# The first 512 rows of x turned by the host, their norm applied at the products' exit; u in four tensors; small tables in one input

## The chip, the cores and the metric

The kernel runs on one core of one Trainium2 chip. A core has a matrix engine (PE, with its weight loads shown apart as PEld), a vector engine (DVE), an activation engine (ACT), a general engine (POOL) and a synchronising engine (SP), which here only issues DMAs. Operands lie in an on-chip memory of 128 partitions; products are summed in eight banks that PE writes and DVE and ACT read. Inputs, the output and scratch tensors lie in the chip's main memory, and DMAs move them.

The metric is the device time of one execution in microseconds (us). The time before is 1565.41 us, the median of three runs (1563.84 to 1569.05).

## The reference

One layer on x (2048 rows of 1024, f32). It is cut here to what the change touches.

```
hn = rmsnorm(x, mix_norm_g)                  # x * rsqrt(mean(x*x) + eps) * g, by row
u, g_ssm, q, k, v, g_attn = split(hn @ w_in) # six times 512 columns
y_ssm = s5(u, a, b, c, d, log_dt) ...        # 32 groups of 16 channels, scanned over the rows
y_ssm = y_ssm * silu(g_ssm)
y_att = stick_breaking(q, k, v) * silu(g_attn)
h = x + concat(y_ssm, y_att) @ w_out
out = h + sigmoid(rmsnorm(h, ple_norm_g) @ w_ple_gate) * (p @ w_ple_proj)
```

The norm of a row is a factor by row, and g is a factor by column of x, that is by row of w_in. So `hn @ w_in` is `rs * (x @ (g * w_in))` with rs the reciprocal root of one row.

## The kernel before, in words

**Split numbers.** A product of f32 accuracy is made of three products in a faster format: each operand is split into a high part (a rounded copy, written by ACT) and a low part (the rest, by DVE), and `mm3` adds high x high, high x low and low x high. `split` does this for activations. `load_w` does it for weights: it loads 128 rows of 512 columns into a staging tile `wst`, multiplies by the column of g (`gmix`) and writes both parts. With `act=True` ACT writes the high part, else DVE.

**First stage, `phase_u`.** The rows are taken in eight units T of 256 rows, each of two tiles of 128. `load_x` brings a tile in by rows (512 KB), ACT squares it and sums by row, DVE and POOL make the reciprocal root (`rms_rstd`; the power is POOL's), ACT scales the tile, PE turns it by 16 transposes of 64 x 64 blocks into two banks, and ACT and DVE split the turned tile into `xt`, which SP also writes out as `hn` (1 MB a tile) for the later stages. `u` of a unit is four column tiles ct of eight row blocks c: 96 products, 24 for each ct. In T = 0 the loop over c is outside, so that products can start with the first weights; in the others ct is outside. ACT copies each finished ct to a tile `uq`, and after each odd T POOL issues one DMA of `uq` (1 MB) to the scratch tensor `u`, laid out as 16 steps x 512 channels x 128 chunks. Two `uq` tiles take turns.

**Tables, `ssm_chain`.** The decay, rotation and power tables of the scan are made from small inputs by some hundreds of short DVE instructions, in the time of the first stage. The inputs come in ten small DMAs on POOL's queue; a and c are turned by PE, halves of b and c are exchanged by ACT.

**Second stage.** Eight batches of the scan (`ssm_pack`, `ssm_batch`; four groups each) run against the gates of the eight units (`gate_unit`, 96 products a unit, units 6 and 7 first since their `xt` are still there) and the first projections of attention (`attn_proj`). A batch reads its channels of `u` by one view, `by_channel`, in the DMA to `us`. As there is one tensor `u`, the first batch's read waits for the last write. From 333 us on come attention and the output, which make up the rest.

**The order of the work** isn't the order of the text. `arrange` takes the whole program, estimates each instruction (`duration`), plans each engine's order by a list schedule with ranks from a backward pass, tries six times, and ties each engine to the best order found. Hints: instructions inside `e.first()` are ranked ahead of all others in the order of the text; DMAs inside `e.later()` don't start before the instruction at `e.mark()` has started, which is the first product of T = 2. Each engine then works strictly in its order: an instruction that waits holds up all behind it on the same engine or queue.

Of the kernel before, what the change touches and what calls it, by code (L numbers as in the profile page):

```python
# [18 lines left out]
P = 128  # L19
# [21 lines left out]
XB, XTB, GTB, QSB, BEB, PXB, WSB, SWB, ROTB, STA, STB, STC, ALT, ALT0, ALT1, SSM_STEPS, SSM_DEPTH, PREP0, BEX, PXX, WSX, XTX, XT0 = 3, 2, 5, 5, 6, 4, 5, 2, 2, 3, 2, 3, "o", 0, 30, 10, 2, 0, 0, 0, 0, 0, 13  # L41
# [8 lines left out]
HOLD = 2  # L50
MATB = 1
GSB = 2
NTAB = 3 * KIN + 3 * MOUT + 1

# [117 lines left out]
def ssm_chain(e, keep, sm):  # L172
# [16 lines left out]
    nre = sm.tile([G, P], F32, tag="nre", name="nre")  # L189
    nim = sm.tile([G, P], F32, tag="nim", name="nim")  # L190
    dma = e.cdma
    ldt = t("ldt")
# [3 lines left out]
    dma(ldt, e.log_dt[0].partition_broadcast(P))  # L196
    dsk = R.dsk = kt("dsk", [G])
    nc.gpsimd.memset(dsk[96:], 0.0)
    lr, li = t("lr"), t("li")
    for src, dst in ((nre, lr), (nim, li)):  # L200
        ps = e.bank("ps_prep", "ssm", "tr")
        nc.tensor.transpose(ps[:, :G], src, e.ident[:G, :G])
        nc.vector.tensor_copy(dst, ps[:, :G])
# [3 lines left out]
    br, bi = (b[0].rearrange("g p h -> p g h") for b in (e.b_re, e.b_im))  # L207
    dma(bst[:ST], br)
    dma(bst[ST:], bi)
    nc.scalar.activation(bsw[:ST], bst[ST:], AF.Copy)  # L210
    nc.scalar.activation(bsw[ST:], bst[:ST], AF.Copy)
    cn1 = sm.tile([P, 4, P], F32, tag="cn", name="cn1")
    cr, ci = (c[0].rearrange("g h p -> (g h) p").rearrange("(k r) p -> r k p", r=P) for c in (e.c_re, e.c_im))
    dma(cn1[:, :, :ST], cr)
    dma(cn1[:, :, ST:], ci)
    dma(dsk[P - GH:], e.d_skip[0].rearrange("g h -> h g"))
    R.cts = kt("cts", [G, GH])
    R.ct2 = kt("ct2", [G, GH])
    ps = e.bank("ps_prep", "ssm", "tr")
    for k in range(4):  # L220
        nc.tensor.transpose(ps[:, k * P:(k + 1) * P], cn1[:, k, :], e.ident)
    c2 = R.ct2.rearrange("p g h -> p (g h)")
    nc.scalar.activation(c2[:ST], ps[ST:], AF.Copy)
    nc.scalar.activation(c2[ST:], ps[:ST], AF.Copy)
    vs(nc, R.cts.rearrange("p g h -> p (g h)"), ps, sgn, ALU.mult)
# [39 lines left out]
    tb = sm.tile([P, G, GH], F32, tag="cn", name="tb")  # L265
# [116 lines left out]

def ssm_batch(e, pool, mb, mc, b):
# [4 lines left out]
    nc.sync.dma_start(us.rearrange("p s k c -> p s (k c)"), by_channel(e.u_d, b))  # L388
# [91 lines left out]
def load_w(e, blocks, width, scale, tag="w", pool=None, bufs=None, at=0, act=True):  # L480
# [67 lines left out]
def phase_u(e, pool, xp, chain):  # L548

    nc = e.nc  # L550

    def load_x(T):
# [17 lines left out]
    with e.first():  # L570
        xts[0] = load_x(0)
        w = load_w(e, row_blocks(e.w_in[0], NC8, 0), 512, e.gmix, act=False)
        xts[1] = load_x(1)
    prep = chain()
    for T in range(NT // 2):
        if 2 <= T + 1 < NT // 2:
            xts[T + 1] = load_x(T + 1)
        xt = xts.pop(T - 2, None)
        xt = xts[T]
        if T % 2 == 0:  # L580
            uq = pool.tile([P, L, 4, NCH // 4], F32, tag="uq", name="uq", bufs=2)
        ps = [e.bank("ps_u", "w0", "w1", "o", "acc")[:, :256] for _ in range(4)]
        if T == 2:
            e.mark()
        for ct, c in [(ct, c) for c in range(NC8) for ct in range(4)] if T == 0 else [(ct, c) for ct in range(4) for c in range(NC8)]:
            cs = slice(ct * P, (ct + 1) * P)
            mm3(e, ps[ct], (w[c][:, 0, cs], w[c][:, 1, cs]), (xt[:, :, 0, c], xt[:, :, 1, c]), c == 0, c == NC8 - 1)
        for ct in range(4):
            k0 = (T % 2) * (NCH // 8)
            nc.scalar.activation(uq[:, :, ct, k0:k0 + NCH // 8], ps[ct].rearrange("p (c j) -> p j c", j=L), AF.Copy)  # L590
        if T % 2 == 1:
            c0 = (T // 2) * (NCH // 4)
            nc.gpsimd.dma_start(e.u_d[:, :, c0:c0 + NCH // 4].rearrange("j (k p) c -> p (j k) c", p=P), uq.rearrange("p j k c -> p (j k) c"))
# [3 lines left out]
def gate_unit(e, pool, w, T, xt):  # L597
# [6 lines left out]
    for ct in range(4):  # L604
        o = e.bank("ps_sg", "o", "z0", "z1")[:, :256]
        for c in range(NC8):
            cs = slice(ct * P, (ct + 1) * P)
            mm3(e, o, (w[c][:, 0, cs], w[c][:, 1, cs]), (xt[:, :, 0, c], xt[:, :, 1, c]), c == 0, c == NC8 - 1)
        sg = pool.tile([P, 256], F32, tag="sg", name="sg", bufs=2)
        nc.scalar.activation(sg, o, AF.Sigmoid)  # L610
# [52 lines left out]
def attn_proj(e, pool, A, i, xt=None):  # L663
# [8 lines left out]
    if len(e.q_banks) == 1:  # L672
# [3 lines left out]
        nc.scalar.activation(flat, pq[:, :384], AF.Copy)  # L676
        nc.vector.tensor_copy(vf, pq[:, 384:])
    else:
# [8 lines left out]
        nc.scalar.activation(part, pq[0], AF.Copy)  # L687
        vt(nc, flat, pq[1][:, :384], part[:, :384], ALU.add)
        vt(nc, vf, pq[1][:, 384:], part[:, 384:], ALU.add)
# [285 lines left out]
def hybrid_block_kernel(ctx: ExitStack, tc: tile.TileContext, x, p, mix_norm_g, w_in, ssm_a_re, ssm_a_im, ssm_log_dt,  # L975
                        ssm_b_re, ssm_b_im, ssm_c_re, ssm_c_im, ssm_d, ssm_w_glu, ssm_b_glu, q_norm_g, k_norm_g,
                        w_out, ple_norm_g, w_ple_gate, w_ple_proj, out, rows, pools, dbg=None):
# [3 lines left out]
    e.x, e.p, e.w_in, e.w_glu, e.w_out, e.w_pg, e.w_pp, e.out = x, p, w_in, ssm_w_glu, w_out, w_ple_gate, w_ple_proj, out  # L981
    e.a_re, e.a_im, e.log_dt, e.d_skip = ssm_a_re, ssm_a_im, ssm_log_dt, ssm_d
    e.b_re, e.b_im, e.c_re, e.c_im = ssm_b_re, ssm_b_im, ssm_c_re, ssm_c_im
# [11 lines left out]
    e.u_d = scratch("u", [L, 512, NCH])  # L995
# [19 lines left out]
    nc.vector.memset(e.mhalf, -0.5)  # L1015

    def column(name, src, n=NC8):
        t = const(name, [P, n])
        nc.sync.dma_start(t, src.rearrange("(c p) -> p c", p=P))
        return t  # L1020

    e.gmix = column("gmix", mix_norm_g[0])

    def late_consts():
        e.gple = column("gple", ple_norm_g[0])
        e.bglu = column("bglu", ssm_b_glu[0])
        e.gqk = const("gqk", [P, 1])
        gk = const("gk", [P, 1])
        for half in range(2):
            d = slice(64 * half, 64 * half + 64)  # L1030
            nc.sync.dma_start(e.gqk[d], q_norm_g[0].unsqueeze(1))
            nc.sync.dma_start(gk[d], k_norm_g[0].unsqueeze(1))
# [40 lines left out]
    e.first, e.later, e.mark = (lambda: hint("first")), (lambda: hint("later")), (lambda: rows.append((len(nc.cur_bb.bb.instructions), 0, "mark")))  # L1073
# [10 lines left out]
    gx = pool(left, "gx")  # L1084
    early = ExitStack()
# [14 lines left out]
    attn_w(e, A[0], 0, NC8)  # L1100
# [405 lines left out]
```

## Time and profile before

| what | us |
|---|---|
| median of three runs | 1565.41 |
| lowest, highest | 1563.84, 1569.05 |
| the profiled execution's own time | 1566.84 |
| its span, first to last instruction | 1565.1 |
| first stage, to the last product of u | 0 to 135.5 |
| second stage, to the last gate product | 135.3 to 332.1 |
| attention and output | 333.5 to 1565.1 |

A row of the timeline has the start, the length, the engine, the source line, the operation, the tile written and the tiles read, the shape and how many were merged; in brackets stands how long the engine was idle before and what ended that. A row of busy time by stretch has the stretch, its length, the busy us of PE, PEld, DVE, ACT and POOL with the number of instructions, PE's granted clock, the DMA engines' mean busy share and GB/s. Products overlap, so a product's length is longer than the step from one to the next: the step is read from the starts.

### The profile page before, as it was taken

What the parts mean: (1) busy time and instruction counts of PE and PEld (TensorE: products, weight loads), DVE (VectorE), ACT (ScalarE), POOL (GpSimd) and SP (SyncE); (2) the same over time, 40 slices, a digit from 0 to 9 for tenths busy, and PEclk for the clock granted to TensorE, in tenths of its full rate; (3) what the DMA queues carried; (4) which work ended last, traced back from release to release, by engine and by line L of the source; (5) the groups of instructions that cost most, each with busy time, mean ns of one, the idle gap of its engine ahead of it and who ended that gap; (6) DMA issues with size and microseconds to landing.
All of it is one profiled execution on the core that took longest, in us unless ns stands there. A gap on an engine that the chain in (4) does not pass through costs nothing.

```text
span 1565.1 us, 34951 instructions
## 1 busy us (share of the span) xinstructions
PE 1484.3 (95%) x13146; PEld 1261.9 (81%) x13146; DVE 1063.4 (68%) x2048; ACT 937.4 (60%) x2074; POOL 813.6 (52%) x1030
## 2 busy tenths in 40 slices
PE   6898999989999999998999988999999999999998
PEld 6898999978888888887788876777776888777776
DVE  7932857967677777677777786656869656754543
ACT  6553545556667877677767777666765435633432
POOL 3150353435456656565666588775555654433433
PEclk9999999999999999999999999999999999999999
DMA  9787735555333422334223365683348655622211
GB/s 303 220 286 190 236 125 175 177 181 170 122 111 111 134 94 90 114 116 135 91 89 115 123 220 168 185 228 102 105 134 269 194 162 181 199 64 94 88 62 61
DMA packets 170697, 235.68 MB, mean 151 GB/s; under 512 B 66256, under 2 KB 112416, under 8 KB 159136
## 3 DMA queue, kind: packets, MB, share of 16 engines
q1 hardware_dynamic: 168272, 225.38, 44.4%
q0 software_dynamic: 2256, 8.06, 2.6%
q8 instruction: 104, 1.70, 0.5%
q14 instruction: 65, 0.53, 0.1%
HBM read 168.51 MB, written 64.90 MB: 149 GB/s over the span
## 4 chain that ended last, share of the span: by engine, by line
PE 73%; DVE 8%; issue 6%; DMA 5%; ACT 4%; POOL 4%; POOLq 0%; SPq 0%; ACTq 0%; DVEq 0%
PE ps_q L685 19%; PE ps_o L784 6%; PE ps_z L745 5%; PE ps_wt L528 4%; PE ps_h L660 3%; PE ps_h L658 3%; PE ps_h L659 3%; PE ps_g L658 3%; PE ps_g L660 3%; PE ps_g L659 3%; DVE px L761 2%; PE ps_g L543 1%; PE ps_sg L543 1%; DMA cs<-in_w_out_dram 1%; PE ps_sg L544 1%
## 5 line engine op out<-in xcount | busy, mean ns | idle before, releaser
L763 POOL TENSOR_TENSOR be<-be,px 128x512 f32<-128x512 f32 (+3 forms) x320 | 316.4, 993 | 208.3 <-DVE px L761 171.9
L685 PE MATMUL ps_q<-w_w,xt 64*128 64x512 f32 x2880 | 407.0, 404 | 11.9 <-DVE v L61 9.8
L761 DVE TENSOR_TENSOR_SCAN px<-px,ps_z 128x512 f32<-128x512 f32 (+3 forms) x320 | 339.8, 1086 | 110.5 <-ACT be L755 78.3
L685 PEld LDWEIGHTS ps_q<-w_w,xt 64*128 64x128 f32 x2880 | 299.0, 187 | 53.7 <-issue 9.0
L750 ACT ACTIVATE px<-ps_z 128x512 f32<-128x512 f32 (+3 forms) x320 | 162.7, 538 | 85.2 <-PE ps_z L745 71.7
L776 ACT ACTIVATE ws<-ps_wt 128x512 f32<-128x512 f32 (+3 forms) x320 | 166.3, 552 | 49.2 <-PE ps_wt L528 48.6
L755 ACT ACTIVATE be<-ps_z 128x512 f32<-128x512 f32 (+3 forms) x320 | 167.8, 554 | 0.5 <-PE ps_wt L528 0.5
L745 PE MATMUL ps_z<-k,q 64*128 64x512 f32 (+3 forms) x960 | 151.0, 384 | 13.7 <-DVE px L761 10.6
L784 PE MATMUL ps_o<-ws,v 128*64 128x128 f32 x2176 | 137.9, 278 | 0.6 <-DVE yat L61 0.6
L784 PEld LDWEIGHTS ps_o<-ws,v 128*64 128x64 f32 x2176 | 118.5, 138 | 18.2 <-issue 14.9
L528 PEld LDWEIGHTS ps_wt<-ident,be 64*128 64x128 f32 x2176 | 104.7, 141 | 27.9 <-issue 9.7
L745 PEld LDWEIGHTS ps_z<-k,q 64*128 64x128 f32 x960 | 97.1, 188 | 36.9 <-DVE px L761 18.3
L528 PE MATMUL ps_wt<-ident,be 64*128 64x64 f32 x2176 | 111.4, 227 | 7.9 <-POOL be L763 3.1
L956 POOL TENSOR_TENSOR sg<-sg,h 128x512 f32<-128x512 f32 x32 | 44.8, 1412 | 114.5 <-DVE sg L61 114.5
L509 POOL TENSOR_TENSOR rs_qk<-rs_qk,mhalf 128x4 f32<-128x4 f32 x64 | 66.1, 1032 | 37.1 <-DVE rs_qk L68 33.9
L543 PE MATMUL ps_u<-xt,w_w 128*128 128x256 f32 x256 | 75.8, 296 | 0.1
L544 PE MATMUL ps_u<-xt,w_w 128*128 128x256 f32 x256 | 75.4, 295 | 0.3 <-DVE xt L61 0.3
L545 PE MATMUL ps_u<-xt,w_w 128*128 128x256 f32 x256 | 75.6, 295 | 0.0
L61 DVE TENSOR_TENSOR yr<-sx,yr 128x512 fp32r<-128x512 f32 x64 | 51.5, 827 | 32.8 <-ACT yr L515 31.8
L515 ACT ACTIVATE yr<-sx 128x512 fp32r<-128x512 f32 x64 | 39.1, 628 | 50.6 <-POOL sx L842 21.9
L759 POOL TENSOR_SCALAR_AFFINE_SELECT px<-px 128x128 f32<-128x128 f32 x128 | 38.7, 312 | 57.4 <-ACT px L750 55.8
L950 ACT ACTIVATE sg<-sg,rs 128x512 f32<-128x512 f32 x24 | 17.4, 723 | 74.3 <-DVE sg L61 74.3
(410 smaller groups left out, 3685.3 us busy)
## 6 DMA issues: line engine op xcount, KB each, us to landing
xt<-hn SPq DMA_DIRECT2D x60, 1024.0 KB, 4.9
hn<-xt SPq DMA_DIRECT2D x16, 1024.0 KB, 9.5
h<-h SPq DMA_DIRECT2D x64, 256.0 KB, 3.9
wst<-in_w_in_dram SPq DMA_DIRECT2D x48, 256.0 KB, 5.5
xg<-hn SPq DMA_DIRECT2D x12, 1024.0 KB, 6.0
x<-in_x_dram SPq DMA_DIRECT2D x16, 512.0 KB, 6.1
out_dram<-sg SPq DMA_DIRECT2D x32, 256.0 KB, 2.5
h<-in_x_dram SPq DMA_DIRECT2D x28, 256.0 KB, 4.5
```

Of the source, the lines that this page charges most:

```text
L528: e.nc.tensor.transpose(ps[h][:, 64 * k:64 * k + 64], v[r], e.ident[r, r])
L543: mm(out, wh, xh, start=first, stop=False)
L658: mm(out, xh, wh, start=first, stop=False, skip_group_check=more)
L659: mm(out, xh, wl, start=False, stop=False, skip_group_check=more)
L685: nc.tensor.matmul(o, xt[r, a, c], A.w[c][r, b], start=c + s == 0, stop=c == NC8 - 1 and s == 2)
L745: nc.tensor.matmul(z[:, :n], q[half[h], a], A.k[ch][half[h], b, :n], start=s == 0, stop=s == 2)
L750: nc.scalar.activation(px[:, :n], z[:, :n], AF.Sigmoid, scale=-(HD ** -0.5))
L755: nc.scalar.activation(be[:, :n], z[:, :n], AF.Sigmoid, scale=HD ** -0.5)
L761: nc.vector.tensor_tensor_scan(rv, rv, z[:, :n][:, ::-1], initial=1.0 if carry[h] is None else carry[h], op0=ALU.mult, op1=ALU.bypass)
L763: nc.gpsimd.tensor_tensor(be[:, :n], be[:, :n], px[:, 1:n + 1], op=ALU.mult)
L776: nc.scalar.activation(dst, ps, AF.Copy)
L784: nc.tensor.matmul(po[half[h], :P], A.v[sb][:, h], w[:, h, b], start=sb == i, stop=sb == 0)
```

## The change

1. The host lays the first 512 rows of x out turned (`xt`: four tiles of 128 x 8 x 128). `load_plain` loads these for T = 0 and 1 in pieces of two row blocks (128 KB), splits them without the norm, and for T = 0 loads the two matching weight blocks in between; ACT writes the weights' high parts now. The last three weights are staged in `uq` tiles, so that no weight load waits for a staging tile.
2. `norms` works out rs of these four tiles: ACT squares the turned tile, POOL adds its eight blocks by halves, a product with ones sums over partitions, POOL takes the power; and a second product spreads rs along a row (`e.row[T]`). The exits multiply by it: u and the gates by the row (DVE), q, k, v by rs as a factor by partition. `hn` of these tiles holds rows without the norm.
3. `u` goes to four tensors of 128 channels, one for each ct, after T = 3 and T = 7, so eight DMAs of 512 KB with runs of 64 numbers in place of four of 1 MB with runs of 32. Columns of w_in are permuted by the host to suit, and a batch reads one of the four tensors (`by_group`). There are four `uq` tiles in place of two of twice the size.
4. All small inputs come in one table (`small`, 128 rows), already turned and exchanged: PE's and ACT's preparation in `ssm_chain` goes.
5. Hints: `later` takes the mark it waits for. T = 1's x waits for the last weight's DMA, `hn` of T = 0 and 1 for the product c = 6 of T = 0, and attention's first weights for T = 2. T = 0 and 1 may use two more banks for their products. XB, the number of x tiles, is 4 for 3.

```diff
-XB, XTB, ... = 3, 2, ...
+XB, XTB, ... = 4, 2, ...
+ACT0 = True
+MARK0, MARK1 = 7, 6
...
-    for k in range(2):
-        dma(nre[:, k * ST:(k + 1) * ST], e.a_re[0])
-        dma(nim[:, k * ST:(k + 1) * ST], e.a_im[0])
...
+    ldt, lr, li = t("ldt"), t("lr"), t("li")
+    for d, name in ((ldt, "log_dt"), (lr, "a_re"), (li, "a_im")):
+        dma(d, e.small(name))
...
+    for d, name in ((bst, "b"), (bsw, "b_turned"), (R.cts, "c"), (R.ct2, "c_turned")):
+        dma(d, e.small(name).rearrange("p (g h) -> p g h", g=G))
+    vs(nc, R.cts, R.cts, sgn, ALU.mult)
...
+def by_group(d, b):
+    n = P // GH
+    return d[b * GB // n].rearrange("(s j) (h g) c -> (j h) s (g c)", s=HS, h=GH)[:, :, b * GB % n * NCH:(b * GB % n + GB) * NCH]
...
-        raw = e.stage[c % len(e.stage)].tile([P, 512], F32, tag="wst", name="wst")[:, :width]
+        if spare is None or c < STB + STA:
+            raw = e.stage[c % len(e.stage)].tile([P, 512], F32, tag="wst", name="wst")[:, :width]
+        else:
+            raw = spare.tile([P, L, NCH // 2], F32, tag="uq", name="wst", bufs=4).rearrange("p j c -> p (j c)")[:, :width]
+        if c == MARK0 and spare is not None:
+            e.mark(0)
...
+    def load_plain(T):
+        xt = xp.tile([P, 2, 2, NC8, P], F32R, tag="xg", name="xt", bufs=2)
+        w = []
+        for hf in range(2):
+            plain.append(pool.tile([P, NC8, P], F32, tag="x", name="x", bufs=XB))
+        for c in range(0, NC8, 2):
+            cs = slice(c, c + 2)
+            for hf in range(2):
+                x = plain[2 * T + hf]
+                nc.sync.dma_start(x[:, cs], e.xt[2 * T + hf, :, cs])
+                split(e, xt[:, hf, 0, cs], xt[:, hf, 1, cs], x[:, cs])
+            if T == 0:
+                w += load_w(e, row_blocks(e.w_in[0], NC8, 0)[cs], 512, e.gmix, act=ACT0, spare=pool, at=c)
+        for hf in range(2):
+            with e.later(1):
+                nc.sync.dma_start(e.hn_d[2 * T + hf], xt[:, hf].rearrange("p s c t -> p (s c t)").bitcast(F32))
+        return xt, w
...
+    def norms(i):
+        x, r = plain[i], e.rs[i]
+        nc.scalar.activation(x, x, AF.Square)
+        for n in (4, 2, 1):
+            nc.gpsimd.tensor_tensor(x[:, :n], x[:, :n], x[:, n:2 * n], op=ALU.add)
+        ps = e.bank("ps_row", "tr", "ssm")
+        nc.tensor.matmul(ps[:, :1], x[:, 0], ones[:, :1], start=True, stop=True)
+        vs(nc, r, ps[:, :1], 1.0 / DM, ALU.mult, EPS, ALU.add)
+        nc.gpsimd.tensor_tensor(r, r, e.mhalf[:, :1], op=ALU.pow)
+        d = pool.tile([P, P], F32, tag="dg", name="dg", bufs=1)
+        vs(nc, d, e.ident, r, ALU.mult)
+        ps = e.bank("ps_row", "tr", "ssm")
+        nc.tensor.matmul(ps[:, :P], ones, d, start=True, stop=True)
+        nc.scalar.activation(e.row[i // 2][:, i % 2 * P:i % 2 * P + P], ps[:, :P], AF.Copy)
...
-        xts[0] = load_x(0)
-        w = load_w(e, row_blocks(e.w_in[0], NC8, 0), 512, e.gmix, act=False)
-        xts[1] = load_x(1)
+        xts[0], w = load_plain(0)
+        norms(0)
+        norms(1)
+        with e.later(0):
+            xts[1], _ = load_plain(1)
+            norms(2)
+            norms(3)
...
-            uq = pool.tile([P, L, 4, NCH // 4], F32, tag="uq", name="uq", bufs=2)
-        ps = [e.bank("ps_u", "w0", "w1", "o", "acc")[:, :256] for _ in range(4)]
+            uq = [pool.tile([P, L, NCH // 2], F32, tag="uq", name="uq", bufs=4) for ct in range(4)]
+        ps = [e.bank("ps_u", "w0", "w1", "o", "acc", *(("z0", "z1") if T < 2 else ()))[:, :256] for _ in range(4)]
...
-            nc.scalar.activation(uq[:, :, ct, k0:k0 + NCH // 8], ps[ct].rearrange("p (c j) -> p j c", j=L), AF.Copy)
-        if T % 2 == 1:
-            c0 = (T // 2) * (NCH // 4)
-            nc.gpsimd.dma_start(e.u_d[:, :, c0:c0 + NCH // 4].rearrange("j (k p) c -> p (j k) c", p=P), uq.rearrange("p j k c -> p (j k) c"))
+            if T < 2:
+                vt(nc, out, o, e.row[T].rearrange("p (c j) -> p j c", j=L), ALU.mult)
+            else:
+                nc.scalar.activation(out, o, AF.Copy)
+            if T % 4 == 3:
+                c0 = (T // 4) * (NCH // 2)
+                nc.gpsimd.dma_start(e.u_d[ct][:, :, c0:c0 + NCH // 2].rearrange("j p c -> p j c"), uq[ct])
...
+        if T < 2:
+            og = pool.tile([P, 256], F32, tag="sg", name="og", bufs=2)
+            vt(nc, og, o, e.row[T], ALU.mult)
+            o = og
...
+        if i < 4:
+            nc.scalar.activation(flat, pq[:, :384], AF.Copy, scale=e.rs[i])
+            vs(nc, vf, pq[:, 384:], e.rs[i], ALU.mult)
...
-    attn_w(e, A[0], 0, NC8)
+    with e.later():
+        attn_w(e, A[0], 0, NC8)
```

More of the change, by code (lines that the diff above doesn't have):

```diff
@@ L1084, in hybrid_block_kernel @@
     gx = pool(left, "gx")
+    e.row = [gx.tile([P, 256], F32, tag=f"row{T}", name=f"row{T}") for T in range(2)]
     early = ExitStack()
@@ L1438, in best_order @@
     hints = [r for r in rows if len(r) == 3]
-    mark = next((a for a, _, kind in hints if kind == "mark"), None)
+    mark = {T: a for a, T, kind in hints if kind == "mark"}
     for a, b, kind in hints:
```

135 lines of the change are left out of this document (71 added, 64 removed).

## The prediction

> **What bounds the kernel now.** I read the whole-page engine line first, then busy time by stretch, then PE's timeline where PE stands still, then the DMA rows of the first stage.
>
> ```profile
> PE 1484.3 (95%) x13146; PEld 1261.9 (81%) x13146; DVE 1063.4 (68%) x2048; ACT 937.4 (60%) x2074; POOL 813.6 (52%) x1030
> ```
> ```profile
> 0.00:17.00 17.00, 3.89 (x39) 3.02 (x39) 7.65 (x23) 8.25 (x13) 9.62 (x19) 1.00 0.92 236
> 17.00:56.00 39.00, 34.66 (x292) 33.08 (x293) 38.06 (x226) 23.40 (x40) 7.17 (x7) 0.92 0.74 251
> 56.00:95.00 39.00, 36.02 (x339) 34.73 (x338) 28.22 (x89) 21.46 (x39) 16.47 (x11) 0.98 0.98 321
> 95.00:135.00 40.00, 39.99 (x362) 39.12 (x362) 11.48 (x17) 19.35 (x35) 10.02 (x8) 0.97 0.73 217
> 135.00:175.00 40.00, 35.60 (x285) 35.40 (x284) 22.37 (x42) 17.51 (x40) 5.74 (x3) 0.91 0.74 196
> ```
> ```profile
> 335.00:1565.00 1230.00, 1178.31 (x10593) 965.84 (x10593) 832.17 (x1434) 764.47 (x1718) 698.46 (x945) 0.99 0.42 135
> ```
>
> The columns are stretch, length, busy PE, PEld, DVE, ACT, POOL, granted clock, DMA share, GB/s. PE sets the time almost everywhere. From 335 us on (attention, output), which the change touches only in a few exits, PE lacks 51.7 us of 1230. What the change can win is PE's standing still, or running slowly, before 175 us: 13 us ahead of 17, about 7 us in the next two stretches, 4.4 after 135. DVE is full (38.06 of 39) from 17 to 56; DMA is full (0.98) from 56 to 95.
>
> ```profile
> 7.75 0.66 DVE L66 TENSOR_SCALAR w_w<-wst,gmix 128x512 fp32r<-128x512 f32 x1
> 14.63 1.12 PE L528 MATMUL ps_x<-ident,x 64*128 64x64 f32 x16 [1.96 <-ACT x L562]
> 16.91 0.58 PE L543 MATMUL ps_u<-xt,w_w 128*128 128x256 f32 x1
> 20.90 0.41 PE L543 MATMUL ps_u<-xt,w_w 128*128 128x256 f32 x1
> 21.11 0.41 PE L544 MATMUL ps_u<-xt,w_w 128*128 128x256 f32 x1
> 26.31 0.71 PE L528 MATMUL ps_x<-ident,x 64*128 64x64 f32 x16
> 27.17 0.28 PE L543 MATMUL ps_u<-xt,w_w 128*128 128x256 f32 x1
> 27.29 0.28 PE L544 MATMUL ps_u<-xt,w_w 128*128 128x256 f32 x1
> 49.98 0.37 PE L528 MATMUL ps_x<-ident,x 64*128 64x64 f32 x1 [3.46 <-DVE xt L61]
> 52.21 0.42 PE L545 MATMUL ps_u<-xt,w_w 128*128 128x256 f32 x1
> 52.42 0.42 PE L543 MATMUL ps_u<-xt,w_w 128*128 128x256 f32 x1
> 92.42 0.71 PE L528 MATMUL ps_x<-ident,x 64*128 64x64 f32 x16 [2.24 <-ACT x L562]
> 154.14 3.78 PE L408 MATMUL ps_b<-us,stB 128*128 128x128 f32 x16 [4.40 <-DMA us<-u]
> ```
>
> The first product with weights starts at 16.91. A product of 256 columns follows the last after 0.12 us when PE is warm (27.17 to 27.29), and after 0.21 us for some 5 us after each start (20.90 to 21.11; 52.21 to 52.42). So each standstill of a few us is paid again in slow products.
>
> **The change part by part, against the profiled execution (1566.84 us; 1565.1 span and 1.7 around it).** It lies 1.43 above the median 1565.41, so what is forecast against it is lowered by 1.4.
>
> ```profile
> 1.29 1.03 SPq L557 DMA_DIRECT2D x<-in_x_dram  x2
> 2.37 2.62 SPq L488 DMA_DIRECT2D wst<-in_w_in_dram  x5
> 5.19 1.06 ACT L560 ACTIVATE jk<-x 128x1024 bf16<-128x1024 f32 x1 [2.90 <-DMA x<-in_x_dram]
> ```
> ```profile
> L515 ACT ACTIVATE xt<-ps_x 128x512 fp32r<-128x512 f32 x32 | 17.4, 596 | 9.5 <-PE ps_x L528 9.5
> L493 ACT ACTIVATE w_w<-wst,gmix 128x512 fp32r<-128x512 f32 x16 | 11.4, 716 | 0.6 <-DMA wst<-in_w_in_dram 0.5
> L72 DVE SCALAR_TENSOR_TENSOR w_w<-wst,gmix,w_w 128x512 fp32r<-128x512 f32 x24 | 19.6, 819 | 21.9 <-ACT w_w L493 21.9
> L61 DVE TENSOR_TENSOR sg<-ps_sg,sg 128x256 f32<-128x256 f32 x14 | 5.8, 417 | 9.0 <-ACT sg L610 8.9
> ```
>
> (1) Start. Square, reciprocal root, scaling and PE transposes leave the path of T = 0; what stays is x, its split, the weight and its split. SP issues x, x, w, w for each pair of row blocks, 0.52 us each (2.62 / 5), so the first weight goes out at about 2.3, as now. The x that goes out at 1.29 is at ACT at 5.19; the first weight is at DVE at 7.75, its landing unknown but before that. Two halves of x on ACT (about 0.4 each, from 596 ns for 512 columns) and the weight's high part (0.72, on ACT now) give a first product between 5.2 + 0.8 + 0.72 = 6.7 and 7.75 + 0.72 + 0.1 = 8.6. I take 7.3: -9.6 (bounds -10.2 and -8.3). Does PE starve afterwards? Sixteen issues end at 1.3 + 16 x 0.52 = 9.6, and 3 MB with 1.1 MB of tables at the 236 GB/s of the first stretch would be there at 19, at the 321 of 56 to 95 at 14. PE wants block 7 after 84 products: 7.3 + 26 x 0.21 + 58 x 0.12 = 19.7. ACT and DVE need some 2.3 us a pair (2 x 0.4 + 2 x 0.72 and 0.4, 0.82 on DVE), PE 2.9 warm. So PE is fed, narrowly at the low rate. The eight DMAs of T = 1's x follow the last weight's on SP (4 us of issue) and have until 22.
>
> (2) The transposes of T = 1 (two groups between products, 0.64 each net of overlap, row 26.31) go: -1.3. The three preparation transposes ran in PE's standstill before 16.91: nothing.
>
> ```profile
> 141.94 1.86 PE L365 MATMUL ps_pack<-cts,bn 128*128 128x16 f32 x16
> 148.89 0.27 PE L359 MATMUL ps_pack<-ident,bn 128*128 128x128 f32 x1
> ```
>
> (3) The norms add to PE eight small f32 products, to ACT four squares (1.06 each) but no scaling, to POOL three sums and a root, to DVE a few short ones. The row comes to T = 0's exit only, 14 us after its first product, so the sums lie under products. On PE: 8 x 0.12 (1.86 / 16) at the least, 8 x 0.27 (one by itself) plus waits of PE's order for POOL at the other end: +1 to +4; I take +1.5. Eight exits move from ACT to DVE (0.42 each, row sg), 3.3 us on the fullest engine.
>
> (4) The stop at 49.98: DVE had the tables' chain in its queue ahead of the split, and PE paid 3.46 idle, then 28 products at 0.21 for 0.12 (2.4) and slower transposes (1.0): 6.9. T = 2 still comes in the old way, and DVE's chain is no shorter (only two copies go), while PE gets there some 11 us sooner with DVE burdened by w's low parts, x's splits and the exits. So the stop may stay whole or go: 0 to -6.9. I take -3. The x of T = 2 also waits for buffers that the norms must release (XB is 4, all taken by the turned x); behind it on SP stand hn's writes and the gate's weights. By ACT's squares at 12 to 14 and POOL's sums (about 2 us a tile) that is free at some 15 to 17, wanted at 22: nothing.
>
> ```profile
> L593 POOL DMA_DIRECT2D u<-uq x4: 2800/2812/2821, 46.6 to 136.3; - x4
> ...
> DMA to landing us min/median/max: 5.4/17.6/18.5
> ```
> ```profile
> 5.96 1.13 POOL L208 DMA_DIRECT2D bst<-in_ssm_b_re_dram  x1
> 90.62 0.56 POOL L509 TENSOR_TENSOR rs_x<-rs_x,mhalf 128x1 f32<-128x1 f32 x1
> ```
> ```profile
> hn<-xt SPq DMA_DIRECT2D x11, 1024.0 KB, 9.7
> x<-in_x_dram SPq DMA_DIRECT2D x8, 512.0 KB, 6.1
> u<-uq POOLq DMA_DIRECT2D x3, 1024.0 KB, 17.9
> ```
>
> (5) u's issue blocks POOL for 2.81 us (8192 runs of 128 B). After, each of eight DMAs has 2048 runs of 256 B: 1.1 by bst's row (2048 runs) to 1.4 by bytes. The root at 90.62, which stood behind such an issue and three table products and cost PE 2.24 idle plus 31 products at about 0.17 for 0.12 (1.6), waits less: 0 to -3.8, I take -1.5.
>
> (6) The tail. Chain of waits:
>
> ```profile
> 136.32 13.71 DMA u<-uq
> 150.13 3.97 DMA us<-u
> ```
> ```profile
> 135.20 0.29 PE L545 MATMUL ps_u<-xt,w_w 128*128 128x256 f32 x1
> ```
>
> The first scan batch reads u only after the last megabyte, issued 0.8 after T = 7's last product. After the change it reads tensor 0 alone, whose columns are done three quarters of a unit (8.6 us) sooner, and half the size. Even at 13.71 it lands 9 us sooner; PE stood 4.40, and its 16 products ran at 0.236 (3.78 / 16) for 0.12 (1.8), the next few slow (0.4). The gate products that cover the wait now (14 us of T = 6) stay. -6, bounds 0 (planner's order puts something else there) and -6.6.
>
> (7) New wait: uq is no longer doubled across DMAs. T = 4's exit into tile k waits until the DMA of T = 0 to 3 has read it; ACT is held, and behind it x's scaling and splits of T = 5. With t the start of T = 3, exit k lies at t + 2.9(k+1), the exit wanted again at t + 12.2 + 2.9(k+1). At half of today's 17.6 the fourth lands at t + 22 against t + 23.8: nothing. At today's time per byte, one after another (14.8 us a MB without the issue), it lands at t + 34: +10. 17.9 us is u's own for 1 MB where hn needs 9.7, so the short runs cost; doubled runs lie nearer the first end: +2. The Trainium skill (DMA: Bandwidth & Descriptors, "Why small descriptors are slow (HBM only)") counts three extra cycles a descriptor, 11 for 256 B and, by the same count, 7 for 128 B: an estimate of 0.79 of today's time per byte, with which this term would be some +4 and the sum 2 us longer; no run yet shows 256 B.
>
> (8) Gates of T = 0 and 1: eight more DVE products (0.42), and og takes one of the two sg buffers, so each column tile waits for the last one's write. PE has scan work between: 0 to +4, I take +1. The scaled exits in attn_proj are one instruction for one; the 17 small table DMAs that become 13 ride beside other work: within (1).
>
> Sum: -9.6 - 1.3 + 1.5 - 3 - 1.5 - 6 + 2 + 1 = -16.9; 1566.84 - 16.9 - 1.4 = 1548.5, **1548 us**. All best: -10.2 - 1.3 + 1 - 6.9 - 3.8 - 6.6 = -27.8, 1538. All worst: -8.3 - 1.3 + 4 + 10 + 4 = +8.4, 1574. The order of every engine is planned anew for the whole program, so attention's 51.7 us of PE idle may shift by a few us either way.
>
> **Rivals.** *A, slow feed:* the blocks of T = 0 come in starts and stops, and all 96 products run at 0.21: 70 x 0.09 = 6.3 more, 1555. For it: DMA at 0.92 moved only 236 GB/s in the first stretch. Against: the tables that moved it in small pieces are now whole rows. The Trainium skill (TensorE: Matmul & The Clock Gate, Part 1) says the clock is halved by default and released by about 3.4 us of sustained work; by that rule gaps between blocks keep it low, and the rows after 16.91 and 49.98 agree that slowness follows a stop.
>
> *B, given back:* PE arrives early where DVE (38.06 of 39) and DMA (0.98) are full, and (4), (5) stay and (7) is 8: -9.6 - 1.3 + 1.5 - 6 + 8 + 1 = -6.4, 1559.
>
> *C, nothing is left:* as B, and the tail stays, since the scan's own latency after u takes the wait's place: 1565. Against: PE is dense from 160 us on.
>
> *D, slower:* u's writes line up on POOL's queue at T = 4. If each lasts d from the first issue at t + 4.3, the last lands at t + 4.3 + 4d, and PE is held by 4d - 19.5. It eats the gain of 18.9 (the sum without (7)) from d = 9.6 on; at 11 us it is +24.5, 1571. For it: 17.6 us for a write today, all on one queue. Against: that was twice the bytes in half the run length.
>
> **How the numbers follow.** Forecast 0.52 (1538 to 1555), A 0.14, B 0.16, C 0.07, D 0.11. A measurement here tells 0.3%, 4.7 us, from no change: faster is below 1560.7, slower above 1570.1. Faster: 0.52 + 0.14 + 0.14 of B = 0.80; same: 0.02 of B, 0.05 of C, 0.02 of D = 0.09; slower: 0.02 of C, 0.09 of D = 0.11. The range takes A and most of B: 1535 to 1563.
>
> **What would show it.** Right: first ps_u product near 7; T = 0's 96 products in some 15 us; no idle ahead of ps_b; the gates begin near 120. Wrong: ACT waiting for a DMA u<-uq at T = 4 (7, D), 0.21 us spacing past 15 us (A), PE waiting for DVE xt between 30 and 60 (4, B). The forecast fails if the attention part, after its first product, changes by more than 5 us.

## The result, and the profile after

| what | before | after |
|---|---|---|
| median of the runs beside each other, us | 1565.09 (1563.84 to 1569.05) | 1578.12 (1576.10 to 1578.93) |
| ratio, 95% interval | | 1.0068 (1.0055 to 1.0081) |
| the profiled execution's own time, its span, us | 1566.84, 1565.1 | 1578.15, 1575.8 |
| last product of u, us | 135.5 | 143.9 |
| first ps_q product of attention, us | 340.7 | 354.9 |
| from that product to the end of the span, us | 1224.4 | 1220.9 |

By the medians the kernel became 13 us slower, where 17 us less were forecast. The last two rows say where: all of the loss is there before attention's projections begin.

Of the page of the kernel after, the engine line; of its trace, busy time by stretch, with the columns of before.

```profile
PE 1489.1 (94%) x13092; PEld 1264.2 (80%) x13092; DVE 1082.3 (69%) x2066; ACT 936.6 (59%) x2074; POOL 821.8 (52%) x1044
```
```profile
0.00:17.00 17.00, 10.23 (x55) 9.55 (x55) 12.72 (x86) 8.77 (x16) 5.25 (x15) 1.00 0.84 279
17.00:56.00 39.00, 27.35 (x193) 25.10 (x193) 33.72 (x155) 20.13 (x36) 16.69 (x20) 0.82 0.70 258
56.00:95.00 39.00, 35.88 (x335) 34.28 (x336) 37.46 (x107) 22.45 (x41) 16.15 (x14) 0.96 0.85 280
95.00:135.00 40.00, 40.00 (x372) 39.20 (x371) 9.24 (x16) 17.18 (x33) 11.99 (x9) 1.00 0.66 232
135.00:175.00 40.00, 40.00 (x342) 40.00 (x342) 24.95 (x47) 21.43 (x46) 6.37 (x6) 1.00 0.77 238
335.00:1575.80 1240.80, 1183.96 (x10644) 970.19 (x10642) 838.07 (x1440) 770.63 (x1730) 698.55 (x947) 0.99 0.42 134
```

The start is won: 55 matrix instructions before 17 us for 39. The stretch after it loses more: 193 for 292, at a granted clock of 0.82 for 0.92. From 135 to 175 the wait ahead of the scan is gone: PE is full. The same view for the products of u alone (columns: stretch, length, busy PE with the count, granted clock, DMA share, GB/s), first before, then after:

```profile
0.00:27.00 27.00, 8.69 (x48) 1.00 0.95 296
27.00:33.00 6.00, 6.00 (x49) 1.00 0.98 374
33.00:42.00 9.00, 7.97 (x67) 1.00 0.57 215
42.00:56.00 14.00, 8.26 (x53) 0.77 0.55 116
```
```profile
0.00:27.00 27.00, 16.15 (x96) 1.00 0.82 284
27.00:33.00 6.00, 0.52 (x2) 0.79 0.70 270
33.00:42.00 9.00, 8.34 (x47) 0.76 0.68 258
42.00:56.00 14.00, 8.88 (x56) 0.76 0.63 227
```

At 27 us the new kernel is 48 products ahead (96 to 48). Six us later the lead is gone (98 to 97), since only two products ran; at 56 us it is 16 behind (201 to 217). PE's timeline of the kernel after shows the places:

```profile
6.35 0.58 PE L535 MATMUL ps_u<-xt,w_w 128*128 128x256 f32 x1 [6.35 <-ACT w_w L485]
18.36 0.62 PE L537 MATMUL ps_u<-xt,w_w 128*128 128x256 f32 x3 [1.53 <-DVE w_w L76]
29.61 0.46 PE L579 MATMUL ps_row<-dg,ones 128*128 128x128 f32 x2 [1.55 <-DVE dg L70]
32.48 0.55 PE L535 MATMUL ps_u<-xt,w_w 128*128 128x256 f32 x1 [2.41 <-DVE uq L65]
41.48 0.71 PE L520 MATMUL ps_x<-ident,x 64*128 64x64 f32 x16
44.62 1.12 PE L520 MATMUL ps_x<-ident,x 64*128 64x64 f32 x16 [2.12 <-DVE pwr L65]
47.15 0.58 PE L535 MATMUL ps_u<-xt,w_w 128*128 128x256 f32 x1 [1.41 <-DVE xt L65]
47.74 0.41 PE L537 MATMUL ps_u<-xt,w_w 128*128 128x256 f32 x1
47.95 0.41 PE L535 MATMUL ps_u<-xt,w_w 128*128 128x256 f32 x1
153.14 1.95 PE L395 MATMUL ps_b<-us,stB 128*128 128x128 f32 x16
203.53 0.77 PE L703 MATMUL ps_qk<-w_w,xg 128*128 128x512 f32 x1 [4.42 <-DVE gsq L65]
```

The first product comes at 6.35, and at 18.36 PE makes its first stop of over 1 us after that, for the low part of a weight. T = 0's last one starts at 25.9, and T = 1's first at 32.48, after an exit of T = 0 (`uq`): it takes the bank that this exit clears. The two extra banks that the change gives to T = 1, z0 and z1, were to spare it just this wait. They went to T = 2's transposes (41.48 and 44.62), and T = 1's other two column tiles began only at 47.15, when T = 2's split had cleared them.

For a measure over time I use PE's loss: the time, less the sum of the usual steps of all matrix instructions started by then (the median step of each group, 0.120 us for a product of u; worked out from the trace). The kernels with the turned x have 2.8 us less of such work in all. Usual steps taken from another kernel shift whole rows, and the 2.8 us with them, by some us; a row's loss and work taken together, that is how far a kernel is ahead of another, move by less than 1 us up to 300 us.

| PE's loss by, us | 24 | 60 | 95 | 160 | 300 | 360 |
|---|---|---|---|---|---|---|
| before | 16.3 | 22.9 | 26.4 | 34.0 | 36.5 | 49.2 |
| after | 13.9 | 28.0 | 32.7 | 32.4 | 44.4 | 62.4 |
| t2_banks | 13.9 | 21.9 | 24.7 | 25.4 | 30.1 | 50.4 |
| t2_chain2 | 7.9 | 14.6 | 22.4 | 23.9 | 29.1 | 50.4 |
| u4_alone | 16.1 | 22.6 | 27.8 | 28.0 | 32.8 | 51.0 |
| no_turned | 19.2 | 23.1 | 25.2 | 26.6 | 29.8 | 48.4 |
| before_chain2 | 15.6 | 15.1 | 22.1 | 31.8 | 36.1 | 49.5 |

### The profile page after: what moved, and what is told of

It reads as the page before. It is cut to its first block, busy times and chain, and to the rows that moved or that the text cites. A ratio compares the mean times of both kernels' runs of the same rounds, so it can differ in the third digit from the quotient of the medians.

```text
span 1575.8 us, 34903 instructions
## 1 busy us (share of the span) xinstructions
PE 1489.1 (94%) x13092; PEld 1264.2 (80%) x13092; DVE 1082.3 (69%) x2066; ACT 936.6 (59%) x2074; POOL 821.8 (52%) x1044
## 4 chain that ended last, share of the span: by engine, by line
PE 73%; DVE 11%; ACT 5%; issue 4%; DMA 3%; POOL 3%; SPq 0%; POOLq 0%; DVEq 0%; ACTq 0%
PE ps_q L734 19%; PE ps_o L838 6%; PE ps_z L799 6%; PE ps_wt L520 4%; PE ps_g L703 3%; PE ps_g L705 3%; PE ps_g L704 3%; PE ps_h L705 3%; PE ps_h L704 3%; PE ps_h L703 3%; DVE px L815 3%; DMA wst<-in_ssm_w_glu_dram 2%; PE ps_sg L535 1%; PE ps_sg L536 1%; PE ps_sg L537 1%
## 5 line engine op out<-in xcount | busy, mean ns | idle before, releaser
L734 PEld LDWEIGHTS ps_q<-w_w,xt 64*128 64x128 f32 x2880 | 294.9, 186 | 50.4 <-issue 9.0
L799 PE MATMUL ps_z<-k,q 64*128 64x512 f32 (+3 forms) x960 | 150.4, 389 | 14.4 <-DVE px L815 13.9
L507 ACT ACTIVATE yr<-sx 128x512 fp32r<-128x512 f32 x64 | 39.3, 628 | 50.3 <-POOL sx L896 19.2
L535 PEld LDWEIGHTS ps_u<-xt,w_w 128*128 128x128 f32 x256 | 52.9, 207 | 11.8 <-ACT w_w L485 7.3
```

Of the source, the lines that this page charges most:

```text
L535: mm(out, wh, xh, start=first, stop=False)
L734: nc.tensor.matmul(o, xt[r, a, c], A.w[c][r, b], start=c + s == 0, stop=c == NC8 - 1 and s == 2)
L799: nc.tensor.matmul(z[:, :n], q[half[h], a], A.k[ch][half[h], b, :n], start=s == 0, stop=s == 2)
```

## The experiments

Each ran beside the kernel before on its chip. The medians of the kernel before were 1565.85 us beside no_turned, u4_alone, t2_banks and pe_sums, 1567.38 beside small_alone, t2_chain, t2_plain_gates and nt_us3, 1566.8 beside t2_chain2, t2_chain4, nt_chain2 and before_chain2, and 1566.4 beside the other two. Times are medians; ratios, with their 95% intervals, are to the kernel before. The order of every engine is planned anew for each.

**The parts of the change.** no_turned leaves the rows to `load_x` as before and keeps the u tensors and the table (with the turned x go the two extra banks, the fourth x tile and the factor at the exits); u4_alone and small_alone put one part into the kernel before.

```diff
-        xts[0], w = load_plain(0)
...
+        xts[0] = load_x(0)
+        w = load_w(e, row_blocks(e.w_in[0], NC8, 0), 512, e.gmix, act=False)
+        xts[1] = load_x(1)
...
-            if T < 2:
+            if False:
```

> The change without the turned x: all rows come in the old way, with their norm ahead of the products; u in four tensors and the table of small inputs stay. If the loss is in the turned x (T = 1 has no bank until T = 0's row is there and T = 2's transposes are read), this is faster than before by the tail's 6 us: about 1559, with no idle ahead of ps_b. If the loss is in u's four tensors, the table or the new order that they bring from 200 us on, it stays at 1572 or more.

> The kernel before with u in four tensors alone. By the step on the tail: 1558 to 1560, first scan products some 5 us sooner, ACT waiting 0 to 2 us for uq at T = 4. By the rival that u's writes line up on POOL's queue: ACT stands 10 us or more at T = 4, and the time is 1570 or more. A gap of over 2 us between this and no_turned is the table's doing.

> The kernel before with the small tables from one host tensor and nothing else of the change. The version without the turned x ran at 0.9970 of the time before and the four u tensors alone at 0.9997, so if the parts add up, the small table is worth 0.27%, 4.2 us: 1561.5. If it is only a different order that the planner found for the two together, this runs within 1.5 us of the time before, 1564.5 to 1567.

no_turned: 1561.65, 0.9970 (0.9958 to 0.9981). u4_alone: 1566.1, 0.9997 (0.9986 to 1.0008). small_alone: 1569.42, 1.0011 (1.0001 to 1.0020). So the turned x carries the whole loss. The four tensors do what step 6 says, the loss from 95 to 160 us is 0.2 instead of 7.6, and yet gain nothing at the end: u4_alone misses its 1558 to 1560. small_alone lies above both of the times that were expected of it. The parts don't add up: alone they bring nothing, together 0.3%. Some 4 us is thus what another order of the whole program may do by itself (no run shows this apart from the edits), and differences of that size between two kernels aren't put down to an edit below.

**The banks, and the row of the norm.** t2_banks gives T = 2's transposes two other banks, tr and ssm; pe_sums replaces POOL's three sums by eight short products that add up in PSUM.

```diff
-            for h, ps in enumerate(turned(e, "ps_x", ("z0", "z1"), ...
+            for h, ps in enumerate(turned(e, "ps_x", ("tr", "ssm") if T == 2 else ("z0", "z1"), ...
```
```diff
-        for n in (4, 2, 1):
-            nc.gpsimd.tensor_tensor(x[:, :n], x[:, :n], x[:, n:2 * n], op=ALU.add)
-        nc.tensor.matmul(ps[:, :1], x[:, 0], ones[:, :1], start=True, stop=True)
+        for c in range(NC8):
+            nc.tensor.matmul(ps[:, :1], x[:, c], ones[:, :1], start=c == 0, stop=c == NC8 - 1)
```

> The change with the transposes of T = 2 in two other banks (tr, ssm), so that the first two column tiles of T = 1 wait for nothing but their operands. If T = 1's wait for banks is the loss: its first product moves from 32.5 to about 26, its last from 55.6 to about 45, and the time falls by 6 to 9 us, to 1569 to 1572. If PE's stop is set by the norms' products, which stand ahead of T = 1 in PE's order, it falls by less than 3.

> The change with the norms' sums over eight blocks made by eight short products on PE in place of three sums on POOL. If the late row (30.5 us) holds T = 1: row 0 comes some 4 us sooner, and DVE, which runs 3 to 7 times longer beside POOL's sums (pr_den 1.28 us for 0.18), is freed: 4 to 6 us faster, 1572 to 1574. If the banks of T = 2 decide, T = 1's second half still starts near 47 and the time moves by less than 2.

t2_banks: 1565.76, 1.0005 (0.9993 to 1.0016), by the medians 12.4 us faster than the changed kernel, by the ratios 0.6%, some 10 us, and more than was expected. pe_sums: 1582.03, 1.0088 (1.0068 to 1.0109). The products of u by stretch in t2_banks, and PE's stops:

```profile
0.00:27.00 27.00, 16.51 (x105) 1.00 0.82 286
27.00:33.00 6.00, 5.66 (x42) 1.00 0.74 281
33.00:42.00 9.00, 7.15 (x48) 1.00 0.67 248
42.00:56.00 14.00, 8.59 (x49) 0.76 0.87 284
```
```profile
29.81 0.39 PE L579 MATMUL ps_row<-dg,ones 128*128 128x128 f32 x2
33.69 0.36 PE L535 MATMUL ps_u<-xt,w_w 128*128 128x256 f32 x1 [0.74 <-DVE uq L65]
46.45 0.58 PE L535 MATMUL ps_u<-xt,w_w 128*128 128x256 f32 x1 [1.11 <-ACT xt L507]
```

The row comes as late as in the changed kernel (29.81 to 29.61), and PE no longer stands for it: 42 products from 27 to 33 us where there were two, 244 by 56 us where there were 201. So it was the banks that held T = 1. By the table 6.1 us of the gain are there by 60 us; another 5 come after 160 us, where the stop at 203.53 is in the changed kernel alone, and these are the new order's rather than the banks'. In pe_sums the row was no earlier (its second half at 30.48), so that run doesn't test the row. It is 4 us slower than the changed kernel by the medians, against both of its expectations, but the intervals overlap, so it doesn't say what POOL's sums cost.

**The factor at the gates.** t2_plain_gates is t2_banks with the gates of T = 0 and 1 left without the norm's factor.

```diff
-        if T < 2:
+        if False:
             og = pool.tile([P, 256], F32, tag="sg", name="og", bufs=2)
```

> The change with T = 2's transposes in two other banks, and the gates of T = 0 and 1 without the norm's factor (left out: eight vector products and the second use of the gates' buffers). Theory 'the factor at the gates costs': up to 4 us less than 1565.8. Rival 'PE has scan work there': within 1 us of 1565.8.

t2_plain_gates: 1565.55, 0.9988 (0.9975 to 1.0001), against 1.0005 (0.9993 to 1.0016) with the factor: the intervals overlap, so 0 to 4 us as step 8 had it, and no more is told.

**What holds T = 2.** Three versions of t2_banks hold the loads of the small tables, and with them the chain of short vector instructions, until late in T = 0 (t2_chain), until T = 2's products (t2_chain2) or T = 4's (t2_chain4); nt_chain2 and before_chain2 do the second in no_turned and in the kernel before.

```diff
-    prep = chain()
+    with e.later(2):
+        prep = chain()
```

> The change with T = 2's transposes in two other banks, and the small tables' loads held until T = 0's products are nearly through (12 products from the end), so that their 1.1 MB and the chain of short vector instructions lie behind the first weights. Theory 'the feed of T = 0 is starved by the tables': its 96 products end at 21 to 23 us instead of 26.2 and the time falls by 3 to 5 us from 1565.8, to 1561 to 1563. Rival 'the stretch is won and paid again when the same vector work meets T = 2's splits at 40 to 50 us': the products end early too, but the stops at 44 and 46 us grow and the time stays within 2 us of 1565.8.

> The change with T = 2's transposes in two other banks, and the small tables' loads held until T = 2's products begin, so that the tables' chain of short vector instructions comes behind T = 2's splits. Theory 'what sets the start of T = 2's products in every version so far (46 to 52 us) is the vector engine, full with that chain': the stops between 36 and 48 us go, T = 2's first product comes at 36 to 40 instead of 46.5, and PE's loss by 60 us falls from 21.9 to 14 to 17 us; if that reaches the end, 1558 to 1561, and if the second stage takes it back as it did with the four u tensors, 1563 to 1566. Rival 'the stop is not the chain's' (x's landing, the norm, the banks): first product of T = 2 still after 44 us, time within 2 us of 1565.8.

> As the version before it, with the tables' loads held until T = 4's products begin. By the theory the first 60 us look the same, or better by up to 2 us (nothing of the chain is left there); the chain then lies under T = 4 to 7, where the vector engine is free (11.5 of 40 us busy from 95 to 135 in the kernel before), but the tables come later, so the scan's first batch may wait: within 3 us of the version before it, slower if ps_b starts after 150 us.

> The change without the turned x, with the tables' loads held until T = 2's products begin. Here the first product stays at about 17 to 18 us, since x is turned on the chip, but the stop at 50 us (2.1 us and slow products after it) should go by the same theory: PE's loss by 60 us 19 to 21 instead of 23.1, time 1558 to 1561 against 1561.7. Rival: no change within 2 us.

> The kernel before with its tables' loads held until T = 2's products begin, nothing else. The theory: the stop of 3.46 us at 50 and its slow products (6.9 us by the prediction's step 4) go, and so does part of the late start; PE's loss by 60 us 14 to 18 instead of 22.9; time 1559 to 1563 against 1565.5, or no change if the second stage takes it back. Rival: loss by 60 us still above 21.

t2_chain: 1566.5, 0.9995 (0.9984 to 1.0006). t2_chain2: 1561.7, **0.9961** (0.9945 to 0.9977). t2_chain4: 1576.83, 1.0051 (1.0036 to 1.0066). nt_chain2: 1562.79, 0.9967 (0.9953 to 0.9981). before_chain2: 1568.74, 1.0006 (0.9994 to 1.0019). In t2_chain T = 0's last product starts at 21.2 instead of 25.9, T = 1's at 36.5, and then PE stands, behind vector work of the tables (`sc_mc`), longer than anywhere else:

```profile
45.47 1.11 PE L520 MATMUL ps_x<-ident,x 64*128 64x64 f32 x16 [8.68 <-DVE sc_mc L72]
```

With the chain behind T = 2's splits, in t2_chain2, that stop goes and T = 2's products begin at 38.80, as the theory said; a smaller one comes later, where the chain then is, and the time lies between the two that were expected:

```profile
38.80 0.58 PE L535 MATMUL ps_u<-xt,w_w 128*128 128x256 f32 x1 [1.15 <-ACT xt L507]
87.28 0.37 PE L520 MATMUL ps_x<-ident,x 64*128 64x64 f32 x1 [5.57 <-DVE xt L65]
```

In before_chain2 the loss by 60 us falls to 15.1, inside what was expected, so the same chain was what held the kernel before at 49.98; in nt_chain2 it falls to 15.4, further than expected. In neither does the time follow: the loss of before_chain2 is 31.8 again by 160 us. t2_chain4 was expected to be slower if the scan began after 150 us; it began at 154.6.

**Work or order in the vector queue.** t2_chain2_rs is t2_chain2 with the short instruction ahead of x's root taken out of the vector queue; t2_chain3 holds the tables until T = 3.

```diff
-            rs = rms_rstd(e, pool, ss, 1, DM, "x")
+            rs = pool.tile([P, 1], F32, tag="rs_x", name="rs_x")
+            nc.gpsimd.tensor_scalar(rs, ss, 1.0 / DM, EPS, op0=ALU.mult, op1=ALU.add)
+            nc.gpsimd.tensor_tensor(rs, rs, e.mhalf[:, :1], op=ALU.pow)
```

> The version with T = 2's transposes in two other banks and the tables held until T = 2's products, and with the multiply and add ahead of x's reciprocal root on POOL instead of the vector engine. In the version without this PE stood 5.57 us at 87.28, and the root of that x had waited for a 128x1 vector instruction that stood in the vector queue behind some fifty of the tables' (85.56, 0.15 us). Theory 'a short instruction in a queue of fixed order is what is late': that stop falls to under 2 us, PE's loss by 95 us from 22.4 to 15 to 18 us; time 1556 to 1560, or no less than 1561 if the second stage takes it back. Rival 'the splits themselves, also on the vector engine, are late': the stop stays above 4 us.

> The version with T = 2's transposes in two other banks and the tables held until T = 3's products begin, one unit later than in the version at 0.9961 and one earlier than in that at 1.0051. Theory: the same vector work meets the splits of one unit later, so PE's loss by 115 us is again 20 to 25 us and the time between the two, 1560 to 1568; if it lies under the splits better, loss by 115 us under 18 and time under 1560.

t2_chain2_rs: 1563.96, 0.9979 (0.9969 to 0.9989). t2_chain3: 1563.64, 0.9980 (0.9967 to 0.9993), loss by 115 us 20.1. In t2_chain2_rs the root is early (79.31, against 85.79 in t2_chain2) and the stop as long, 5.97 us at 89.31. My theory fell: it is the splits, the work itself, that stand behind the chain, and moving the chain moves the stop.

**The end of the second stage.** nt_us3 is no_turned with three buffers for the scan's u instead of two.

```diff
-    us = pool.tile([P, HS, GB, NCH], F32, tag="us", bufs=SSM_DEPTH, name="us")
+    us = pool.tile([P, HS, GB, NCH], F32, tag="us", bufs=3, name="us")
```

> The change without the turned x, with three buffers for the scan's u instead of two, so that the load of u of batch b no longer waits for the products of batch b - 2. Theory 'the second stage ends when the scan's chain of batches ends, and a batch is held by its u buffer': the last ps_y product comes 3 us or more ahead of 323.8 and the time falls from 1561.7 to 1557 to 1559. Rival 'the chain is held by the vector work and the order of PE, not by the buffers': last ps_y within 2 us of 323.8, time within 2 us of 1561.7.

nt_us3: 1563.13, 0.9972 (0.9963 to 0.9982); the last ps_y product at 324.7 against 324.0: the buffers don't hold the chain of batches. What takes the gains back shows in part in the gate products among PE's groups from 300 to 345 us (line, engine, operation, tile, shape, count | busy us, mean ns | idle us before them and what ended it), before and then t2_banks:

```profile
L545 PE MATMUL ps_sg<-xg,w_w 128*128 128x256 f32 x49 | 13.9, 284 | 0.0
```
```profile
L537 PE MATMUL ps_sg<-xg,w_w 128*128 128x256 f32 x36 | 10.3, 285 | 0.0
```

Before, gate products run beside the scan's last batch to its end (last gate product 331.8, last ps_y 328.5). In t2_banks the gates are through at 313.0 and the last ps_y is at 325.2: the gates came earlier and the scan didn't by as much, so PE has nothing to lay over the last batch. The first ps_q product follows the last ps_y by 12.3 to 13.8 us in both kernels of the case, in t2_banks, u4_alone and no_turned. In these three the loss was 6 to 9 us below that of before at 160 us, and is within 2 of it at 360. What holds the scan's batches isn't settled; their buffers don't.

## Why the prediction was wrong

About half of the miss lies on each side of 160 us. By then the kernel has won 4.4 us (a loss 1.6 below that of before, and 2.8 of work), where the terms of the sum that lie there add up to 17.9; from there on it loses 14.8 us more than before, where the sum had 1.

**The step that failed** first is (3), "the row comes to T=0's exit only, 14 us after its first product, so the sums lie under products", and with it a term that the sum lacked: what T = 1 waits for. The row came at 30.5, 5 us after T = 0's last product and not under its products. Behind that stand POOL's sums, which waited for ACT's squares (at 19.63 instead of 12 to 14), these in turn for a split by the vector engine, and at the end ACT's copy:

```profile
19.63 1.06 ACT L569 ACTIVATE x<-x 128x1024 f32<-128x1024 f32 x1 [3.31 <-DVE xt L65]
20.78 4.69 POOL L571 TENSOR_TENSOR x<-x 128x512 f32<-128x512 f32 x4 [14.55 <-ACT x L569]
30.26 0.26 ACT L580 ACTIVATE row<-ps_row 128x128 f32<-128x128 f32 x1
```

That alone would have cost little, as t2_banks shows. But `load_x` of T = 2 stands in the text ahead of T = 1's banks, so z0 and z1 went to T = 2 first, and T = 1 had nothing to run on. It was in the code to be read, and the prediction costed the two extra banks at nothing without naming their next user. With T = 2's transposes elsewhere the kernel is at 1.0005, and 6.1 us of that gain are there by 60 us.

**(1) Start.** First product at 6.35, better than 7.3. But 96 products took from 6.35 to 25.9, not some 15 us. The blocks came in starts and stops, as rival A had it, though the products ran at 0.21 only up to 13.3. DMA and the vector engine were both full while the weights were on their way, in the kernel after:

```profile
12.00:16.00 4.00, 4.00 (x30) 3.95 (x29) 4.00 (x24) 3.25 (x7) 0.00 (x0) 1.00 1.06 375
```

Two stops of PE after that were the vector queue's and not the DMAs':

```profile
17.56 0.75 DVE L76 SCALAR_TENSOR_TENSOR w_w<-wst,gmix,w_w 128x512 fp32r<-128x512 f32 x1
20.59 1.32 ACT L485 ACTIVATE w_w<-wst,gmix 128x512 fp32r<-128x512 f32 x2
```

At 18.36 PE had waited for the low part that the vector engine began at 17.56, behind short instructions of the tables, though ACT had written its high part by 15.7. At 21.35 it had waited 0.70 us for a high part that ACT began at 20.59, behind the norm's square that had waited for the vector engine; the last two weights had landed at 16.5 and 17.2. That the tables' 1.1 MB and their vector work (DVE 4.00 of 4) come in the same 10 us was given no price. t2_chain, without these, ends T = 0 4.7 us sooner.

**(4)** was the other wrong size. The stop at 49.98 was given -3 on the grounds that it may stay or go. It is set by the vector engine, not by when PE arrives: T = 2's first product is at 51.62 before, 46.45 in t2_banks and 47.76 in t2_chain, though PE was through with T = 1 at 36.8 there. Whatever is won ahead of it is worth at most what T = 2 gains, some 5 us, until the chain is moved. That is the mechanism of rival B, which has PE arrive early where DVE is full. The x of T = 2 went out at 24.72, where (4) had its buffers free at 15 to 17; no run shows whether that cost anything.

**(2)** holds as far as shown: no transposes of T = 0 and 1. **(5)** POOL's issue fell as forecast, 1.18 for 2.81, and no stop of PE between 56 and 135 us ends with ACT's scaling any more, but nothing of it is seen in the sum: busy PE from 56 to 95 is 35.88 for 36.02. In u4_alone, which has the short issue and the old x, PE stood 3.67 us at 90.00 for that scaling; the root had waited there for the vector engine and not for an issue.

```profile
L634 POOL DMA_DIRECT2D u<-uq x8: 1154/1176/1219, 74.7 to 145.0; - x8
...
DMA to landing us min/median/max: 4.9/8.8/11.6
```

**(6)** was right: no idle ahead of ps_b (153.14), and the loss from 95 to 160 us is -0.3 instead of 7.6. The gain didn't stay: u4_alone has it too and ends at 0.9997. **(7)** was nothing rather than +2; ACT waited for no DMA of u at T = 4, and rival D fell. The landings mix two cases: the four writes after T = 3 were under way together and took 10.4 to 11.6 us each, the four after T = 7 took 4.9 to 7.3. What a byte costs shows in the time of the DMA packets on POOL's queue (packets, MB, share of 16 engines' span), before and then in u4_alone, which moves the same bytes and differs in u alone:

```profile
q0 software_dynamic: 2256, 8.06, 2.6%
```
```profile
q0 software_dynamic: 2320, 8.06, 1.9%
```

The 1024 packets of 4 KB that carried u took 422 ns each on average before, 254 in u4_alone and 270 in the kernel after, 0.60 and 0.64 of it. The factor of 0.79 that the prediction worked out from the Trainium skill (DMA: Bandwidth & Descriptors, "Why small descriptors are slow (HBM only)") has the right direction and is too weak by these packets. **(8)** stays unresolved, within its 0 to 4.

**After 160 us** the sum had +1; the loss there grew by 14.8 us more than in the kernel before (62.4 - 32.4 against 49.2 - 34.0). 6 us of it lie at 203.53 (loss 33.4 by 200 us, 39.4 by 220). The vector and POOL rows ahead of that stop are these:

```profile
189.85 0.22 DVE L65 TENSOR_TENSOR lags<-lags,dg 32x64 f32<-32x64 f32 x1
190.10 1.23 DVE L65 TENSOR_TENSOR bn<-bn,tm 128x1024 f32<-128x1024 f32 x1
194.76 2.12 DVE L65 TENSOR_TENSOR dg<-ident,dsk 32x64 f32<-32x64 f32 x1
196.89 3.46 DVE L65 TENSOR_TENSOR tm<-pwis,bbs 128x1024 f32<-128x1024 f32 x1
200.27 0.68 DVE L76 SCALAR_TENSOR_TENSOR gsq<-gsq,ps_y 128x512 f32<-128x512 f32 x1
```
```profile
194.75 2.04 POOL L332 TENSOR_TENSOR stC<-pwr,cts 128x1024 f32<-128x1024 f32 x1
196.87 2.39 POOL L334 TENSOR_TENSOR stC<-stC,tm 128x1024 f32<-128x1024 f32 x1
```

The vector instructions at 194.76 and 196.89 took 2.12 and 3.46 us, where like shapes took 0.22 and 1.23 just before: each is longer by about the length of the POOL instruction that began 0.01 to 0.02 us ahead of it. And `gsq`, for which PE waited, stood behind them. Such meetings are in the kernel before too (two of its `bn` instructions took 2.93 and 3.08 us for 1.22), but only here does PE wait so long behind one: no other kernel of this document has PE idle for more than 2.2 us at once from 160 to 300 us. The order that puts them there is new with the change. The prediction allowed a few us either way for attention's order and nothing for the second stage's. The other 9 us are lost in t2_banks as well (25.4 to 50.4, against 34.0 to 49.2 before), whose last batch of the scan has no gate products beside it; why the batches don't come sooner stays open.

**A version that beats both** is t2_chain2, at 0.9961 (0.9945 to 0.9977); no_turned, without the turned x, reaches 0.9970 (0.9958 to 0.9981), so the turned x is worth nothing measurable even when repaired.

## What to carry to other kernels

When a unit starts sooner, ask for each buffer or bank it is given who takes it next in the order of the text, and for the first thing that doesn't start sooner with it (here an engine full with other work at 45 us); the gain can't be larger than what that point moves. A wait removed ahead of a long, full stage is worth something only if the work at the end of the stage can come sooner too; compare the last instructions of its parallel parts before adding the gain up. In a kernel whose order is planned as a whole, two edits that are each worth nothing can be worth 4 us together, so effects of that size need a run, not a sum.

## What the runs showed of the hardware that had not been expected

In these rows a vector instruction with two operands in on-chip memory waits for the whole of a POOL instruction that began just before it: 128x32 took 1.28 us in place of 0.18 when the first of POOL's sums, 1.27 us long, began 0.03 us ahead of it.

```profile
20.78 1.27 POOL L571 TENSOR_TENSOR x<-x 128x512 f32<-128x512 f32 x1 [14.55 <-ACT x L569]
19.95 0.18 DVE L65 TENSOR_TENSOR sc_s<-sc_s,sc_r 128x32 f32<-128x32 f32 x1
20.81 1.28 DVE L65 TENSOR_TENSOR pr_den<-pr_t,pr_t 128x32 f32<-128x32 f32 x1
```

The Trainium skill (SBUF — State Buffer, "SBUF: two separate sides") says that the two engines share one pair of ports under an exclusive lock held for the whole instruction; the rows here and at 194 us agree. The prediction laid the norm's sums on POOL at no cost to the vector engine, which was already full there.

After the stops of 2.41 us at 32.48 and of 2.12 and 1.41 us ahead of 47.15 the products ran at 0.21 for 0.12 us (47.74 to 47.95 above) for some 4 us, so such a stop costs more than its idle time; this the prediction had from the kernel before. It isn't so after every stop: behind the 1.53 us at 18.36 they ran at 0.12 at once (18.82 to 18.94).
